# Attention logits in two row halves, with the forget-gate bias and the causal mask in one tile

## The chip, the cores and the metric

The kernel runs on one core of one Trainium2 chip, as one program launched once. The metric is the device time in microseconds of one execution; times are medians of several runs. One further execution is recorded by the hardware profiler, and all rows below are from such executions.

## The reference

A decoder of two layers over 256 tokens of width 1024, all in float32. Each layer is a feed-forward at half step, a token mixer and another feed-forward at half step, with RMSNorm in front of and behind each. The mixer of the first layer is a gated linear recurrence. That of the second is "forgetting" attention with 16 heads of 64, whose keys, values and gates are computed from the stream between the layers:

```python
def shared_kv(h, g, w_kv, w_f, b_f):
    hn = rms_norm(h, g)
    kv = (hn @ w_kv)            # keys and values, 16 heads of 64
    log_f = log_sigmoid(hn @ w_f + b_f)
    c = cumsum(log_f, axis=1)   # running sum over the tokens, per head
...
    logits = q @ k + c[query] - c[key]
    logits = where(key <= query, logits, -inf)
    p = softmax(logits)
    o = p @ v
```

## The kernel before

The 256 tokens are two row tiles of 128, called t = 0 and t = 1. Every large product splits both operands into a high and a low part and adds three products of the parts (lines L183 to L185). The high part of a weight is an ACT copy (L173), the low part a DVE subtraction (L177). The weights arrive through the SP queue into five `raw` buffers, and nine pairs of split buffers (`WB = 9`) let the splits run ahead of PE.

The work is a list of items, each with a `prep` (load and split) and a `work` (the products for one row tile). `slot(t, i)` does item i for tile t. `run` walks the list, tile 1 some `LAG = 7` slots behind tile 0. `ahead(i, fn)` makes item i's prep call `fn` first. `defer(n, fn)` calls `fn` n slots later. PE's instructions stay in the order in which they are written. The other engines' order is settled when the program is built, by a planner that takes what is ready first, by its own estimates; on the chip each of them then works through its list in order. `keep_in_program_order` pins an instruction behind the one written before it on the same engine.

The stages that the change touches, in the order of time:

- Between the layers, keys, values and gates. `post_f` makes the log gates `lf`. Fifteen slots later `running(t)` sums them on PE with a triangle of ones, with heads on partitions: `c` is 16x128. A DMA lays `c` into row 65 of the key tile `kT`, whose row 64 is ones. `heads_T` scales the 512 columns of a projection (`htok`, L954), two slots later transposes them four times (L959), and copies the lower 64 partitions by ACT (L962) and the upper 64 by DVE (L963), so that every head lies on partitions 0 to 63.
- The first feed-forward of the second layer. Its last items are the 22 rows of the down projection. Its gate and up products use two buffers with the tag `sil`. At its end, `enter` computes the norm: sums of squares on ACT, `rstd` on POOL (L198, L200), the new `h` on DVE (L285), and PE's transposes of `h` (L214).
- The attention. `att_rows` lays `c` and minus one into rows 64 and 65 of the query tiles `qT`, by four POOL DMAs (L947, L948), so that a product of 66 rows holds query times key plus both running sums. The steps of the attention are laid by hand between the slots of the query and output projections (`ATT_ORDER`): `l` logits, `n` norm, `t` transposes (L1084), `v` values (L1098), each followed by its row tile. One `l` does a group of heads that fills one of two `gt` PSUM banks: four heads of 128 keys for tile 0, two of 256 for tile 1 (L1063). DVE adds the mask to the diagonal block (L1064) and takes the maximum (L1066), ACT takes the exponential head by head with its sum (L1071).

A float32 product of these small ones goes through PE in two passes, so the row counts of L1063 are twice the number of products.

Of the kernel before, what the change touches and what calls it, by code (L numbers as in the profile page):

```python
# [23 lines left out]
NRT = 11  # L24
NH = 16
HD = 64
HA = HD + 2
EPS = 1e-6
RAW = 5
WB = 9  # L30
# [14 lines left out]
def trunk_kernel(ctx: ExitStack, tc: tile.TileContext, A: dict, out: bass.AP):  # L45
# [6 lines left out]
    hpool = ctx.enter_context(tc.tile_pool(name="h", bufs=1))  # L52
    spool = ctx.enter_context(tc.tile_pool(name="small", bufs=4))
    psum = ctx.enter_context(tc.tile_pool(name="psum", bufs=1, space=bass.MemoryType.PSUM))

    uid = [0]

    def nm(s):
        uid[0] += 1
        return f"{s}_{uid[0]}"  # L60
# [4 lines left out]
    def gtbank():  # L65
        return psum.tile([P, 512], F32, tag="gt", name=nm("gt"), bufs=2)
# [850 lines left out]

    def kv_tiles():
        lp = ctx.enter_context(tc.tile_pool(name="kv", bufs=1, reuse_waits="tile"))
        kv["kT"] = lp.tile([HA, NH, S], F32, name="kT")  # L920
        kv["v"] = [lp.tile([P, D], F32, name=f"v{t}") for t in range(2)]

        kv["lf"] = [lp.tile([P, NH + 8], F32, name=f"lf{t}")[:, :NH] for t in range(2)]
        kv["c"] = [lp.tile([NH, P], F32, name=f"c{t}") for t in range(2)]
        kv["bfb"] = lp.tile([P, NH], F32, name="bfb")
        for n in ("triu", "mone", "cmask"):
            kv[n] = lp.tile([P, P], F32, name=n)

    def kv_constants():

        keep = tc.keep_in_program_order
        triu, cm = kv["triu"], kv["cmask"]
        keep(nc.gpsimd.dma_start(kv["bfb"], A["b_fgate"].partition_broadcast(P)))
        keep(nc.gpsimd.memset(triu, -1.0))
        keep(nc.gpsimd.affine_select(out=triu, in_=triu, compare_op=ALU.is_ge, fill=0.0, base=0,
                                     pattern=[[1, P]], channel_multiplier=-1))
        keep(nc.gpsimd.memset(kv["mone"], -1.0))
        keep(nc.gpsimd.memset(cm, 0.0))
        keep(nc.gpsimd.affine_select(out=cm, in_=cm, compare_op=ALU.is_ge, fill=NEG, base=0,
                                     pattern=[[-1, P]], channel_multiplier=1))  # L940
        keep(nc.gpsimd.memset(kv["kT"][HD:HA, :, :], 1.0))
# [8 lines left out]
    def heads_T(pool, ps, t, n, scale, dst):  # L950

        tok = pool.tile([P, 512], F32, tag="prod", name=nm("htok"), bufs=2)
        with tc.high_priority():
            nc.vector.tensor_scalar(tok, ps, rs[t][:, 0:1], scale, ALU.mult, ALU.mult)  # L954

        def turn():
            tp = trbank()
            for j in range(4):
                nc.tensor.transpose(tp[:, j * P:(j + 1) * P], tok[:, j * P:(j + 1) * P], ident)  # L959
            to = dst[:HD, 8 * n:8 * n + 8, :].rearrange("p (a two) b -> p a two b", two=2)  # L960
            with tc.high_priority():
                nc.scalar.activation(to[:, :, 0, :], tp[:HD, :].rearrange("p (a b) -> p a b", a=4), AF.Copy)  # L962
                nc.vector.tensor_copy(to[:, :, 1, :], tp[HD:, :].rearrange("p (a b) -> p a b", a=4))  # L963
        defer(2, turn)

    def post_k(n):
        return lambda t, ps: heads_T(pools["f"], ps, t, n, 1.0, kv["kT"][:, :, t * P:(t + 1) * P])

    def post_f(t, ps):
        fp = pools["f"]  # L970
# [15 lines left out]
        rest()  # L986

    def running(t):
        pc = gtbank()
        if t == 1:  # L990
            nc.tensor.matmul(pc[:NH, :P], kv["lf"][0], kv["mone"], start=True, stop=False)
        nc.tensor.matmul(pc[:NH, :P], kv["lf"][t], kv["triu"], start=t == 0, stop=True)
        nc.vector.tensor_copy(kv["c"][t], pc[:NH, :P])
        nc.gpsimd.dma_start(kv["kT"][HD + 1:HA, :, t * P:(t + 1) * P], kv["c"][t])

    def z_x(t, k):
        return zx[t][0][:, k, :], zx[t][1][:, k, :]
# [33 lines left out]
    for n in range(2):  # L1031
# [11 lines left out]

    def att_tiles():
        ap = pools["a"]
        att["q"] = [ap.tile([HA, NH, P], F32, name=f"qT{t}") for t in range(2)]
        att["oh"] = [ap.tile([P, 8, P], F32R, name=f"oh{t}") for t in range(2)]
        att["ol"] = [ap.tile([P, 8, P], F32R, name=f"ol{t}") for t in range(2)]

    def attention(t):  # L1050

        ap = pools["a"]
        nk = t + 1
        per = 4 // nk
        mask = kv["cmask"].unsqueeze(1).to_broadcast([P, per, P])
        box = {}
        G = NH // per

        def logits(hg):
            hds = range(hg * per, (hg + 1) * per)  # L1060
            ps = gtbank().rearrange("p (a b) -> p a b", a=per)
            for j, hd in enumerate(hds):
                nc.tensor.matmul(ps[:, j, :], att["q"][t][:, hd, :], kv["kT"][:, hd, :nk * P], start=True, stop=True)  # L1063
            nc.vector.tensor_tensor(ps[:, :, t * P:], ps[:, :, t * P:], mask, ALU.add)  # L1064
            mx = spool.tile([P, 4], F32, tag="mx", name=nm("mx"))
            nc.vector.tensor_reduce(mx[:, :per], ps, AX.X, ALU.max, negate=True)  # L1066
            if hds[0] % 8 == 0:
                box["sm"] = spool.tile([P, 8], F32, tag="sm", name=nm("sm"))
            pe = ap.tile([P, per, nk * P], F32, tag="pe", name=nm("pe"), bufs=3)
            for j, hd in enumerate(hds):  # L1070
                nc.scalar.activation(pe[:, j, :], ps[:, j, :], AF.Exp, bias=mx[:, j:j + 1],  # L1071
                                     accum_out=box["sm"][:, hd % 8:hd % 8 + 1])
            box["pe", hg], box["s", hg] = pe, box["sm"][:, hds[0] % 8:hds[0] % 8 + per]

        def norm(hg):
            pe, sm = box["pe", hg], box["s", hg]
            nc.vector.reciprocal(sm, sm)
            nc.vector.tensor_tensor(pe, pe, sm.unsqueeze(2).to_broadcast([P, per, nk * P]), ALU.mult)

        def turn(hg):  # L1080
            tp = trbank()
            pev = box["pe", hg].rearrange("p a b -> p (a b)")
            for j in range(4):
                nc.tensor.transpose(tp[:, j * P:(j + 1) * P], pev[:, j * P:(j + 1) * P], ident)  # L1084
            pT = box["pT", hg] = ap.tile([P, 4, P], F32, tag="pT", name=nm("pT"), bufs=4)
            nc.scalar.activation(pT.rearrange("p a b -> p (a b)"), tp, AF.Copy)

        def values(hg):

            hds = range(hg * per, (hg + 1) * per)  # L1090
            if hds[0] % 8 == 0:
                box["po"] = mmbank()
            po, pT = box["po"].rearrange("p (a b) -> p a b", a=4), box["pT", hg]
            for j in range(0, per, 2):
                for k in range(nk):
                    for s in range(2):
                        hd = hds[j + s]
                        nc.tensor.matmul(po[s * HD:(s + 1) * HD, hd % 8 // 2, :], kv["v"][k][:, hd * HD:(hd + 1) * HD],  # L1098
                                         pT[:, (j + s) * nk + k, :], start=k == 0, stop=k == nk - 1)
            if hds[-1] % 8 == 7:  # L1100
                b = hds[-1] // 8
                oh_v = att["oh"][t][:, 4 * b:4 * b + 4, :].rearrange("p a b -> p (a b)")
                ol_v = att["ol"][t][:, 4 * b:4 * b + 4, :].rearrange("p a b -> p (a b)")
                nc.scalar.activation(oh_v, box["po"], AF.Copy)
                nc.vector.tensor_tensor(ol_v, box["po"], oh_v.bitcast(F32), ALU.subtract)

        return {c: [lambda i=i, f=f: f(i) for i in range(G)] for c, f in zip("lntv", (logits, norm, turn, values))}

    def post_q(n):
        return lambda t, ps: heads_T(pools["a"], ps, t, n, HD ** -0.5, att["q"][t])  # L1110

    for n in range(2):
        proj_items(A["attn_w_q"][0], n * 512, 512, main_x, post_q(n))
# [246 lines left out]
```

## Time and profile before

| | |
|---|---|
| median of three runs | 987.53 us (987.33 to 987.55) |
| the profiled execution | 987.51 us, its span 985.8 us |
| granted clock of TensorE | 0.998 |
| busy: PE, DVE, ACT, POOL | 978.0, 616.6, 530.1, 47.2 us |
| DMA, mean over the span | 193 GB/s, 190.45 MB |

A row of a view gives the line of the kernel, the engine, the operation, the tiles (out<-in), shapes and times; "x8" is a count, and the bracket at the end is the engine's idle time before it and what ended it. PE is matmul, PEld the weight load that overlaps it, DVE the vector engine, ACT the scalar engine, POOL GpSimd, SP the queue that issues most DMAs. In the chain of work, a piece has its start, its length up to the next piece, the engine and the line. A row of the table of windows has, for each engine, busy time and count, then the granted clock, the share of the DMA engines and GB/s. A row of the DMA queues has packets, MB and the share of 16 engines' span. A row of the DMA issues has KB and the median time from issue to landing.

### The profile page before, as it was taken

To read this page: it belongs to the slowest core of one execution; us is meant where nothing else is said; L and a number is where in the kernel's file an instruction comes from. 1 tells how busy PE (TensorE), PEld (TensorE's weight loads), DVE (VectorE), ACT (ScalarE), POOL (GpSimd) and SP (SyncE) were. 2 spreads that over 40 slices of the span, in tenths; PEclk is the share of its full clock that TensorE was granted. 3 is DMA by queue.
4 is the path that set the end of the run, shared out by engine and by line. 5 is a ranking of instruction groups with operands and counts; after the bars stand their busy time and mean duration, and the time that the engine had idled before them with its cause. 6 is when DMAs were issued, how large, how long until landed. Compare 5 with 4: busy or idle time off the path is not lost.

```text
span 985.8 us, 13028 instructions
## 1 busy us (share of the span) xinstructions
PE 978.0 (99%) x4777; PEld 813.4 (83%) x4777; DVE 616.6 (63%) x791; ACT 530.1 (54%) x753; POOL 47.2 (5%) x92
## 2 busy tenths in 40 slices
PE   9999999999999999999999999999999999999997
PEld 6888888898978888888898888888888788888886
DVE  6666554678997555554686655554488876555542
ACT  7545443568986544443564444544366755444431
POOL 2400000100003000000100000000020000000000
PEclk9999999999999999999999999999999999999999
DMA  8787766565346877666567676665552467776631
GB/s 292 263 266 249 222 210 192 158 192 162 117 126 198 241 211 212 217 207 188 131 203 242 186 220 213 214 213 185 190 173 64 123 210 235 213 213 212 205 117 43
DMA packets 99558, 190.45 MB, mean 193 GB/s; under 512 B 12734, under 2 KB 32614, under 8 KB 99494
## 3 DMA queue, kind: packets, MB, share of 16 engines
q1 hardware_dynamic: 98054, 188.95, 61.3%
q8 instruction: 38, 0.62, 0.3%
q10 hardware_dynamic: 608, 0.53, 0.2%
q0 software_dynamic: 832, 0.12, 0.1%
q14 instruction: 26, 0.21, 0.1%
HBM read 176.95 MB, written 1.05 MB: 181 GB/s over the span
## 4 chain that ended last, share of the span: by engine, by line
PE 98%; issue 1%; DVE 1%; ACT 0%; POOL 0%; POOLq 0%; DVEq 0%; ACTq 0%
PE mm L183 29%; PE mm L185 29%; PE mm L184 28%; PE gt L761 2%; PE tr L525 1%; PE mm L1195 1%; PE gt L1063 1%; PE mm L190 1%; PE mm L191 1%; PE mm L192 1%; PE mm L1098 1%; PE tr L1084 1%; PE gt L214 1%; PE tr L127 0%; PE tr L959 0%
## 5 line engine op out<-in xcount | busy, mean ns | idle before, releaser
L177 DVE TENSOR_TENSOR wlo<-raw,whi 128x1024 fp32r<-128x1024 f32 (+5 forms) x329 | 395.3, 1207 | 268.3 <-ACT whi L173 266.1
L173 ACT ACTIVATE whi<-raw 128x1024 fp32r<-128x1024 f32 (+5 forms) x329 | 341.9, 1046 | 314.8 <-PE mm L185 260.2
L183 PE MATMUL mm<-whi,xhi 128*128 128x512 f32 (+1 forms) x768 | 301.2, 392 | 0.0
L185 PE MATMUL mm<-whi,xlo 128*128 128x512 f32 (+1 forms) x768 | 298.2, 388 | 0.3 <-DVE xlo L228 0.3
L184 PE MATMUL mm<-wlo,xhi 128*128 128x512 f32 (+1 forms) x768 | 297.9, 388 | 0.0
L185 PEld LDWEIGHTS mm<-whi,xlo 128*128 128x128 f32 x768 | 144.2, 188 | 30.7 <-DVE xlo L228 0.7
L183 PEld LDWEIGHTS mm<-whi,xhi 128*128 128x128 f32 x768 | 144.2, 188 | 29.4 <-issue 1.3
L184 PEld LDWEIGHTS mm<-wlo,xhi 128*128 128x128 f32 x768 | 144.3, 188 | 28.2 <-DVE wlo L177 0.3
L183 PE MATMUL mm<-whi,hhi 128*128 128x512 f32 x352 | 137.9, 392 | 0.0
L185 PE MATMUL mm<-whi,hlo 128*128 128x512 f32 x352 | 137.1, 389 | 0.0
L184 PE MATMUL mm<-wlo,hhi 128*128 128x512 f32 x352 | 137.0, 389 | 0.0
L185 PEld LDWEIGHTS mm<-whi,hlo 128*128 128x128 f32 x352 | 66.1, 188 | 13.9
L184 PEld LDWEIGHTS mm<-wlo,hhi 128*128 128x128 f32 x352 | 66.1, 188 | 13.3
L183 PEld LDWEIGHTS mm<-whi,hhi 128*128 128x128 f32 x352 | 66.1, 188 | 13.3
L510 DVE SCALAR_TENSOR_TENSOR prod<-mm,rstd,sil 128x512 f32<-128x512 f32 (+1 forms) x48 | 33.8, 705 | 35.2 <-PE mm L185 31.1
L498 ACT ACTIVATE sil<-mm,rstd 128x512 f32<-128x512 f32 (+1 forms) x48 | 31.2, 651 | 38.7 <-PE mm L185 34.2
L198 POOL TENSOR_SCALAR nv<-ss 128x1 f32<-128x1 f32 x22 | 9.6, 435 | 716.3 <-ACT junk L205 716.3
L529 ACT ACTIVATE hhi<-tr 128x512 fp32r<-128x512 f32 (+1 forms) x48 | 24.8, 558 | 13.8 <-PE tr L525 13.8
L205 ACT ACTIVATE junk<-mm 128x512 bf16<-128x512 f32 x24 | 14.3, 595 | 32.7 <-PE mm L185 32.6
L272 DVE TENSOR_TENSOR t<-mm,gb 128x512 f32<-128x512 f32 x24 | 16.1, 685 | 24.7 <-ACT junk L205 24.6
L530 DVE TENSOR_TENSOR hlo<-tr,hhi 128x512 fp32r<-128x512 f32 (+1 forms) x48 | 29.2, 640 | 2.6 <-ACT hhi L529 2.6
L183 PE MATMUL mm<-whi,zhi 128*128 128x340 f32 (+2 forms) x80 | 28.2, 353 | 0.0
(196 smaller groups left out, 885.8 us busy)
## 6 DMA issues: line engine op xcount, KB each, us to landing
raw<-in_ffn_w_down_dram SPq DMA_DIRECT2D x88, 512.0 KB
raw<-in_ffn_w_up_dram SPq DMA_DIRECT2D x80, 512.0 KB
raw<-in_ffn_w_gate_dram SPq DMA_DIRECT2D x78, 512.0 KB
prr<-prod SPq DMA_DIRECT2D x40, 256.0 KB
raw<-in_rg_w_in_dram SPq DMA_DIRECT2D x10, 504.0 KB
raw<-in_rg_w_out_dram SPq DMA_DIRECT2D x10, 504.0 KB
raw<-in_ffn_w_gate_dram SPq DMA_DIRECT2D x19, 256.0 KB
raw<-in_ffn_w_up_dram SPq DMA_DIRECT2D x16, 256.0 KB
```

Of the source, the lines that this page charges most:

```text
L173: up = nc.scalar.activation(hi[:parts, c:c + m], rawv[:, c:c + m], AF.Copy)
L177: nc.vector.tensor_tensor(lo[:parts, c:c + m], rawv[:, c:c + m], hi[:parts, c:c + m].bitcast(F32), ALU.subtract)
L183: nc.tensor.matmul(ps, xh, wh, start=first, stop=False)
L184: nc.tensor.matmul(ps, xh, wl, start=False, stop=False)
L185: nc.tensor.matmul(ps, xl, wh, start=False, stop=last)
L205: nc.scalar.activation(junk[:, :src.shape[1]], src, AF.Square, scale=f, accum_out=acc)
L272: nc.vector.tensor_tensor(t1[n], pf[n], gb[:, n * 512:(n + 1) * 512], ALU.mult)
L498: nc.scalar.activation(s[:, :nn], ps, AF.Silu, scale=rs[t][:, 0:1])
L510: nc.vector.scalar_tensor_tensor(pr[:, :nn], ps, rs[t][:, 0:1], s, ALU.mult, ALU.mult)
L529: nc.scalar.activation(hv, tp[:, :nn], AF.Copy)
L530: nc.vector.tensor_tensor(lv, tp[:, :nn], hv.bitcast(F32), ALU.subtract)
L761: nc.tensor.matmul(ps[j][:w, g * S:(g + 1) * S], wv[rows, o:o + w], xc[rows, k, :], start=start, stop=stop, skip_group_check=True)
```

## The change

Keys and queries stay as the transposes leave them: two heads on the two halves of the 128 partitions, copied once by ACT. A product of logits has 64 rows, and the even heads (rows 0 to 63) and odd heads (64 to 127) go to two PSUM banks. One `l` step does two groups, the next one nothing. Mask and running sums are no longer in the product: they are a bias tile, added when the maximum is taken, in one DVE instruction per head that also writes the (negated) sum to SBUF for the exponential.

For that, `running` computes the sums a second time with tokens on partitions (`cq`) and writes the sums with heads on partitions to DRAM (`rows`). A bias over four heads and 128 keys is made by three steps: a POOL DMA spreads four of these rows over all partitions, DVE subtracts `cq`, and for a diagonal block POOL puts the mask in. The bias of tile 0 is made in `running(0)` and stays in SBUF. That of tile 1 (2 MB) is made in eight parts in the tail of the feed-forward in front of the attention, in the two `sil` buffers, and each part is written to DRAM; `att_rows` loads all of it by one DMA.

```diff
     def kv_tiles():
-        kv["kT"] = lp.tile([HA, NH, S], F32, name="kT")
+        kv["kT"] = lp.tile([P, NH // 2, S], F32, name="kT")
...
+        kv["cq"] = [lp.tile([P, NH], F32, name=f"cq{t}") for t in range(2)]
+        kv["bias0"] = lp.tile([P, NH, P], F32, name="bias0")
+        kv["rows"] = dram.tile([NH, S], F32, name="crows")
+        kv["bias1"] = dram.tile([P, NH, S], F32, name="bias1d")
...
+    def bias_of(v, t, h0, masked):
+        nc.vector.tensor_tensor(v, v, kv["cq"][t][:, h0:h0 + 4].unsqueeze(2).to_broadcast([P, 4, P]), ALU.subtract)
+        if masked:
+            tc.keep_in_program_order(
+                nc.gpsimd.affine_select(out=v, in_=v, compare_op=ALU.is_ge, fill=NEG, base=0,
+                                        pattern=[[0, 4], [-1, P]], channel_multiplier=1))
+
+    def key_rows(v, h0, k):
+        tc.keep_in_program_order(nc.gpsimd.dma_start(v, kv["rows"][h0:h0 + 4, k * P:(k + 1) * P].partition_broadcast(P)))
+
+    def bias_part(i):
+        h0, k = i // 2 * 4, i % 2
+        def f():
+            v = pools["f"].tile([P, 512], F32, tag="sil", name=nm("bp"), bufs=2).rearrange("p (a b) -> p a b", a=4)
+            key_rows(v, h0, k)
+            bias_of(v, 1, h0, k == 1)
+            tc.keep_in_program_order(nc.gpsimd.dma_start(kv["bias1"][:, h0:h0 + 4, k * P:(k + 1) * P], v))
+        return f
...
     def att_rows():
-        for t in range(2):
-            tc.keep_in_program_order(nc.gpsimd.dma_start(att["q"][t][HD:HD + 1, :, :], kv["c"][t]))
-            tc.keep_in_program_order(nc.gpsimd.dma_start(att["q"][t][HD + 1:HA, :, :], kv["mone"][:NH, :]))
+        tc.keep_in_program_order(nc.gpsimd.dma_start(att["bias1"], kv["bias1"]))
...
     def heads_T(...):
-                nc.scalar.activation(to[:, :, 0, :], tp[:HD, :].rearrange("p (a b) -> p a b", a=4), AF.Copy)
-                nc.vector.tensor_copy(to[:, :, 1, :], tp[HD:, :].rearrange("p (a b) -> p a b", a=4))
+                nc.scalar.activation(dst[:, 4 * n:4 * n + 4, :], tp.rearrange("p (a b) -> p a b", a=4), AF.Copy)
...
     def running(t):
...
+        if t == 1:
+            nc.tensor.matmul(pq[:, :NH], one, kv["lf"][0], start=True, stop=False)
+        nc.tensor.matmul(pq[:, :NH], kv["triu"], kv["lf"][t], start=t == 0, stop=True)
...
+        nc.vector.tensor_copy(kv["cq"][t], pq[:, :NH])
+        nc.gpsimd.dma_start(kv["rows"][:, t * P:(t + 1) * P], ct)
+        if t == 0:
+            for h0 in range(0, NH, 4):
+                key_rows(kv["bias0"][:, h0:h0 + 4, :], h0, 0)
+                bias_of(kv["bias0"][:, h0:h0 + 4, :], 0, h0, True)
...
+    for i in range(8):
+        ahead(n_ffn3 - 10 + i, bias_part(i))
...
         def logits(hg):
-            hds = range(hg * per, (hg + 1) * per)
-            ps = gtbank().rearrange("p (a b) -> p a b", a=per)
-            for j, hd in enumerate(hds):
-                nc.tensor.matmul(ps[:, j, :], att["q"][t][:, hd, :], kv["kT"][:, hd, :nk * P], start=True, stop=True)
-            nc.vector.tensor_tensor(ps[:, :, t * P:], ps[:, :, t * P:], mask, ALU.add)
-            nc.vector.tensor_reduce(mx[:, :per], ps, AX.X, ALU.max, negate=True)
+            if hg % 2:
+                return
+            ps = [gtbank() for _ in range(2)]
...
+            for hd in range(h0, h0 + 2 * per):
+                r = slice(hd % 2 * HD, (hd % 2 + 1) * HD)
+                nc.tensor.matmul(logit(hd), att["q"][t][r, hd // 2, :], kv["kT"][r, hd // 2, :w], start=True, stop=True,
+                                 skip_group_check=True)
...
+            for g in (hg, hg + 1):
+                for j, hd in enumerate(hds):
+                    nc.vector.tensor_tensor_reduce(pe[:, j, :], logit(hd), bias[:, hd, :], -1.0, -NEG, ALU.add, ALU.min,
+                                                   mx[:, j:j + 1])
+                for j, hd in enumerate(hds):
+                    nc.scalar.activation(pe[:, j, :], pe[:, j, :], AF.Exp, bias=mx[:, j:j + 1], scale=-1.0,
+                                         accum_out=box["sm"][:, hd % 8:hd % 8 + 1])
```

More of the change, by code (lines that the diff above doesn't have):

```diff
@@ L26 @@
 HD = 64
-HA = HD + 2
 EPS = 1e-6
@@ L925, in kv_tiles @@
         kv["bfb"] = lp.tile([P, NH], F32, name="bfb")
-        for n in ("triu", "mone", "cmask"):
-            kv[n] = lp.tile([P, P], F32, name=n)
+        kv["triu"] = lp.tile([P, P], F32, name="triu")
+        kv["one"] = lp.tile([P, 32], F32, name="one")[:, :1]
+        kv["bias0"] = lp.tile([P, NH, P], F32, name="bias0")
+        kv["rows"] = dram.tile([NH, S], F32, name="crows")
+        kv["bias1"] = dram.tile([P, NH, S], F32, name="bias1d")
     def kv_constants():
         keep = tc.keep_in_program_order
-        triu, cm = kv["triu"], kv["cmask"]
+        triu = kv["triu"]
@@ L933, in kv_constants @@
         keep(nc.gpsimd.dma_start(kv["bfb"], A["b_fgate"].partition_broadcast(P)))
-        keep(nc.gpsimd.memset(triu, -1.0))
+        keep(nc.gpsimd.memset(triu, 1.0))
         keep(nc.gpsimd.affine_select(out=triu, in_=triu, compare_op=ALU.is_ge, fill=0.0, base=0,
                                      pattern=[[1, P]], channel_multiplier=-1))
[L937 to L940, printed above, removed]
@@ L941, in kv_constants @@
-        keep(nc.gpsimd.memset(kv["kT"][HD:HA, :, :], 1.0))
+        keep(nc.gpsimd.memset(kv["one"], 1.0))
+    def bias_of(v, t, h0, masked):
[4 more added lines that the diff above has]
+                                        pattern=[[0, 4], [-1, P]], channel_multiplier=1))
@@ L953, in heads_T @@
+    def heads_T(pool, ps, t, n, scale, dst, tag, bufs):
+        tok = pool.tile([P, 512], F32, tag=tag, name=nm("htok"), bufs=bufs)
         with tc.high_priority():
@@ L1045, in att_tiles @@
         ap = pools["a"]
-        att["q"] = [ap.tile([HA, NH, P], F32, name=f"qT{t}") for t in range(2)]
+        att["q"] = [ap.tile([P, NH // 2, P], F32, name=f"qT{t}") for t in range(2)]
+        att["bias1"] = ap.tile([P, NH, S], F32, name="bias1")
         att["oh"] = [ap.tile([P, 8, P], F32R, name=f"oh{t}") for t in range(2)]
@@ L1054, in attention @@
         per = 4 // nk
-        mask = kv["cmask"].unsqueeze(1).to_broadcast([P, per, P])
+        bias = kv["bias0"] if t == 0 else att["bias1"]
+        w = nk * P
         box = {}
```

34 lines of the change are left out of this document (17 added, 17 removed).

## The prediction

> **What bounds the kernel now.** I read the page's busy times and its chain of work first, then the pieces of that chain in the attention and around the steps that the change moves, then the rows of DVE and POOL there.
>
> ```profile
> span 985.8 us, 13028 instructions
> PE 978.0 (99%) x4777; PEld 813.4 (83%) x4777; DVE 616.6 (63%) x791; ACT 530.1 (54%) x753; POOL 47.2 (5%) x92
> PE 98%; issue 1%; DVE 1%; ACT 0%; POOL 0%; POOLq 0%; DVEq 0%; ACTq 0%
> ```
>
> TensorE (PE) is busy for 978.0 of 985.8 us and 98% of the chain is PE. So a change gains only what it takes off PE's own queue. It loses whatever PE has to wait for, because PE works in order and nothing is slack behind it. The profiled execution took 987.51 us, 1.7 more than its span, and the median of the three timed runs is 987.53: the sum below can be made against either.
>
> **What the row halves take off PE.** In the chain, one group of logits (L1063) of the first row tile is 8 passes over 128 columns, one of the second is 4 passes over 256.
>
> ```profile
> 738.49 0.89 PE gt L1063 x8
> 760.50 0.44 PE tr L1084 x4
> 765.45 0.86 PE gt L1063 x4
> 766.31 1.02 PE mm L1098 x16
> 767.34 0.59 PE tr L1084 x4
> ```
>
> A whole pass takes 0.111 us (0.89/8) or 0.215 us (0.86/4). The price of half-height passes is in the same trace twice. The values (L1098) use two column halves: 16 passes of 128 columns take 1.02 us, 0.064 each, and the transposes behind them 0.59 in place of 0.44. The gates of the first layer (L761) use two row halves, as the change does, on 256 columns:
>
> ```profile
> 221.01 2.79 PE gt L761 x16
> 223.80 0.43 PE mm L183
> 224.23 0.23 PE mm L184
> ```
>
> Eight of these 16 passes are whole (8 x 0.215 = 1.72), eight are halves. Of 2.79 us, and 0.20 that the next matmul is late (0.43 for 0.23), the halves have 1.27 us.
>
> After the change two groups run in one call. A call for the first row tile has 16 half passes of 128 columns: 1.02 + 0.15 = 1.17 us against 2 x 0.89 = 1.78, so 0.61 saved, and there are two calls: 1.2 us. A call for the second tile has eight half passes of 256 columns, just L761's eight: 1.27 against 2 x 0.86 = 1.72, so 0.45 saved, times four calls: 1.8 us. Together 3.0 us.
>
> **What the running sums add to PE.** They are computed a second time with tokens on partitions: one fp32 product of 16 columns for tile 0 and two for tile 1, six passes.
>
> ```profile
> 529.89 0.32 PE gt L991 x2
> L1063 PEld LDWEIGHTS gt<-kT,qT x64: 186/190/192, 734.4 to 776.1; 66*128 66x128 f32 x64
> ```
>
> No row has so few moving columns against 128 stationary ones. If only the moving columns count, a pass is an eighth of 0.11 us, 0.1 in all; if the weight load is bare, it is 0.19, 1.1 in all. I take the pace of small fp32 passes, 0.11 (0.44/4 for L1084): 0.7 us. **PE's own sum is 3.0 - 0.7 = 2.3 us off: 985.2 us**, with bounds 984.6 and 985.6 from these prices.
>
> **DVE and ACT in the attention.** Mask add and maximum go; one fused instruction per head comes.
>
> ```profile
> L1064 DVE TENSOR_TENSOR gt<-gt,cmask x12: 410/432/699, 735.8 to 776.8; 128x256 f32<-128x256 f32 x8, 128x512 f32<-128x512 f32 x4
> L1066 DVE TENSOR_REDUCE mx<-gt x12: 666/683/691, 736.5 to 777.8; 128x2 f32<-128x512 f32 x8, 128x4 f32<-128x512 f32 x4
> L1071 ACT ACTIVATION_READ_ACCUMULATOR pe<-gt,mx x32: 192/200/224, 737.6 to 779.4; 128x1 f32 x32
> L963 DVE COPY qT<-tr x4: 692/693/693, 734.1 to 763.8; 64x512 f32<-64x512 f32 x4
> 740.00:750.00 10.00, 10.00 (x65) 8.48 (x64) 9.06 (x13) 6.45 (x21) 0.00 (x0) 1.00 0.44 121
> ```
>
> Gone: 4 x (0.70 + 0.68) + 8 x (0.43 + 0.68) = 14.4 us and four copies of qT, 2.8 us. The fused instruction is not in the trace. As one pass like L1064's it is 0.30 on 128 columns (the line through 0.43 and 0.70) and 0.43 on 256: 16 x 0.30 + 16 x 0.43 = 11.7 us. If its sum is read out separately, as ACT's is in 0.20, it is 18.1. So DVE, 9.06 busy of 10 us here, ends between 5.5 us lighter and 0.9 heavier. I take the lighter half, since two PSUM passes become one, and no PE time. The exponentials read SBUF for PSUM, count unchanged; both banks are free sooner because the exponentials no longer hold them. A DVE that is heavier instead is a rival below. The kT and qT copies on ACT keep their size in columns; nothing waits for the DVE halves any more.
>
> **What the bias tile adds in front.** This is where I see the danger. Eight parts each do: a POOL DMA that spreads four rows of 128 over 128 partitions (256 KB), a DVE subtraction, for every second part a POOL select over 128x512, and a POOL DMA of 256 KB to DRAM. All of a part's POOL instructions are pinned behind the ones before. So part i+1 cannot ask for its rows until part i's have landed and DVE is through. One round is a full DMA latency, and eight rounds are serial. Their rows:
>
> ```profile
> bfb<-in_b_fgate_dram POOLq DMA_DIRECT2D x1, 8.0 KB, 4.2
> qT<-c POOLq DMA_DIRECT2D x2, 8.0 KB, 5.8
> q1 hardware_dynamic: 98054, 188.95, 61.3%
> q10 hardware_dynamic: 608, 0.53, 0.2%
> L994 POOL DMA_DIRECT2D kT<-c x2: 490/546/603, 520.1 to 531.0; - x2
> L935 POOL TENSOR_SCALAR_AFFINE_SELECT triu<-triu x1: 990/990/990, 312.7 to 312.7; 128x128 f32<-128x128 f32 x1
> ```
>
> A small POOL DMA lands in 4.2 us (a broadcast) to 5.8. The part's 512 packets of 512 B are 32 for each of 16 DMA engines. A packet takes 0.10 us on the big queue (61.3% of 16 x 985.8 us by 98054) and 0.05 on the small one: 1.7 to 3.2 us more. The landing is then 5.9 to 9.0 us. With a subtraction of 0.69 (L1064's 128x512 form), an issue of 0.5 and half a select (0.99 for 128 columns; up to four times that for 512), a round is 7.6 to 12.2 us. I take 7.6: the queues stand at 0.6 here.
>
> The rows use the gate buffers (tag sil, two of them), which this layer's last gate product reads until here:
>
> ```profile
> 667.59 0.48 DVE L510 SCALAR_TENSOR_TENSOR prod<-mm,rstd,sil 128x256 f32<-128x256 f32 x1 [0.73 <-ACT sil L498]
> 687.43 1.23 DVE L177 TENSOR_TENSOR wlo<-raw,whi 128x1024 fp32r<-128x1024 f32 x1 [1.50 <-ACT whi L173]
> 690.15 1.23 DVE L177 TENSOR_TENSOR wlo<-raw,whi 128x1024 fp32r<-128x1024 f32 x1 [1.49 <-ACT whi L173]
> 714.39 0.30 POOL L198 TENSOR_SCALAR nv<-ss 128x1 f32<-128x1 f32 x1 [182.85 <-ACT junk L205]
> 714.77 0.56 POOL L200 TENSOR_TENSOR rstd<-nv,mhalf 128x1 f32<-128x1 f32 x1
> 715.37 1.42 DVE L285 SCALAR_TENSOR_TENSOR h<-t,rstd,h 128x512 f32<-128x512 f32 x2 [0.36 <-POOL rstd L200]
> 717.59 0.87 PE gt L214 x8
> ```
>
> From 668.1 us, eight rounds of 7.6 end at 729. But at 714.4 POOL has to compute rstd of tile 0 (L198, L200). DVE's h (L285) waits for that, and PE's transposes (L214) for h: h is done at 716.79, PE starts at 717.59. That chain has 0.80 us to spare. Two things are queued behind a late part: on POOL the rstd, and on DVE the low halves of the weights (L177), since DVE too works in an order fixed at build. L177 comes every 2.72 us, after 1.5 us of idle time, and of the nine split buffers about five lie between tile 0 and tile 1, so the splits run some four units ahead of PE: an estimate of 11 us of cover. So DVE's queue can bear one late part but not a growing lag; POOL's rstd can bear 0.8 us.
>
> How many parts stand in front of the rstd in POOL's queue is the planner's choice, which no row shows. None gives 0; all eight give 729 - 714.4 - 0.8 = 13.8 us. I take one round, since rounds are long and the planner can only put the rstd between two of them: 7.6 - 0.8 = 6.8 us. **The sum is 985.2 + 6.8 = 992.0 us.**
>
> The rest I cost at nothing. Four such rounds for tile 0's bias run on POOL from 520 us; their DVE steps could hold up the key projection:
>
> ```profile
> 542.07 0.75 DVE L954 TENSOR_SCALAR htok<-mm,rstd 128x512 f32<-128x512 f32 x1 [0.40 <-PE mm L185]
> 544.76 0.44 PE tr L959 x4
> 753.17 0.86 PE gt L1063 x4
> ```
>
> The htok that PE transposes is done 1.9 us ahead; a subtraction waiting for its rows longer than that would add the excess, at most a round. The one 2 MB load of the bias is issued after 726 in place of four small ones. At the page's mean of 193 GB/s it is about 11 us long, and its first reader follows the logits at 753: covered, unless the last part is later than about 738.
>
> **A rule against my forecast.** The Trainium skill, "DMA: Bandwidth & Descriptors", section "Anatomy of one DMA — SWDGE (gpsimd) path", gives such a DMA 2.0 us plus its bytes over 436 GB/s: an estimate of 2.6 us for 256 KB. By it a round would be 4.3 us, the eight would end at 702, and the sum would be 985.2. The rows here have 4.2 to 5.8 us for 8 KB alone, so I go by them.
>
> **The rivals.** *The gain comes through: 985.2 us.* If 256 KB land as fast as the 8 KB broadcast (4.2 us), a round is 5.9 us and eight end at 715, just as the rstd is wanted. Or the planner sees the rounds as long as they are and puts the rstd and the weights first; then only the load at 738 remains as a limit. The point that decides is a landing of 4.2 us, or POOL's order. For it: DVE and ACT have idle time in this stretch. Against it: every POOL DMA in the trace is at 4.2 us or above when other queues move. The skill's fit above falls under this rival.
>
> *All parts stand in front: 999 us and above.* Eight rounds of 7.6 give 985.2 + 13.8 = 999.0; rounds of 8.1 give 1003. For it: between 572 and 714 POOL has nothing else, so nothing stops the planner from starting early.
>
> *The attention eats it: 987.5 us.* If the fused instruction costs 0.20 more, DVE is 0.9 us heavier where it is 9.06 of 10 busy, and transposes wait; a loss of 2.3 us would balance PE's gain. The same result would follow if the two row halves did not run side by side; L761 speaks against that.
>
> **How the numbers follow.** The forecast has 0.42, the gain that comes through 0.36, all parts in front 0.15, the eaten gain 0.07. About 0.2% (2 us) is what a measurement here can tell from no change. Of the rival at 985.2, whose bounds reach 985.6, 0.33 lies below 985.55 and is faster; 0.03 of it and the eaten gain are the same, 0.10; the rest is slower, 0.57. The forecast by itself reaches from 988 (half a round late) to 998. The range goes to both sides of that, from 984.4, just under the gain that comes through, to 1003, so that the slowest rounds alone are left out.
>
> **What would show it.** Right: L1063 at about 1.2 us a call in place of 1.7 to 1.8; landings of the rows at 6 us or more; a DVE subtraction that waits for a DMA; rstd later than 715 and idle time of PE at L214, or at a split, worth about 7 us. Wrong: landings near 4 us, or rstd in time with parts behind it. Then PE stays at 99% without a gap and the time is near 985. PE idle in the attention with DVE full would mean the fused instruction.

## The result and the profile after

The changed kernel takes 1015.51 us (median of 4 runs, 1014.43 to 1016.2); the kernel before took 987.54 beside it. The ratio is 1.0282, with a 95% interval of 1.0264 to 1.03. The forecast was 992.0, with a range of 984.4 to 1003.0: the direction is right, the size is outside the range.

The profiled execution took 1015.15 us. From its page, in this order: span, busy times, the granted clock in 40 slices of the span, and the chain that ended last.

```profile
span 1013.3 us, 13121 instructions
...
PE 985.0 (97%) x4783; PEld 813.3 (80%) x4783; DVE 617.0 (61%) x837; ACT 531.0 (52%) x753; POOL 69.8 (7%) x114
...
PEclk9999999999999999999998999999889999999999
...
PE 85%; issue 6%; DMA 4%; DVE 2%; POOL 1%; ACT 1%; POOLq 0%; DVEq 0%; ACTq 0%
```

The span is 27.5 us longer. PE's share of the chain falls from 98% to 85%: DMA, issue and DVE are on it now. And the clock line, 9 throughout before, has three slices of 8, one in the key projection and two near the end of the feed-forward. Three stages of work move the time. I compared the start of the same product (every L183, counted from the first) in both traces: at the last product ahead of the key projection the changed kernel is 0.7 us late, behind that projection 10.9, where the attention begins about 30.6, and at the end 27.6. So: **+10.2 in the key projection, +19.7 in the tail of the feed-forward, -3.0 in the attention.** (The running sums have 0.2 of the first 0.7 us and 0.5 of the 10.2.)

The waits of the changed kernel that are new or longer (engine, line, what it waited for: us in total, times, longest):

```profile
DVE bp L944 <- DMA bp<-crows: 24.0, 5, 5.9
POOL bias1d L960 <- DVE bp L944: 22.6, 4, 6.1
DVE bias L944 <- DMA bias<-crows: 17.3, 4, 5.7
DVE bp L944 <- issue: 15.8, 3, 5.4
PE mm L184 <- DVE wlo L177: 10.6, 3, 6.5
PE tr L977 <- DVE htok L972: 7.7, 2, 5.6
```

The first and third lines are the new subtraction standing on DVE until its rows have landed. The fourth is the same subtraction in the three other rounds of the tail; the profile shows no releaser for them, but they are as long as the rest. In the tail that makes eight waits, 39.8 us. The last two are PE standing for DVE: for the low halves of weights (L177) in the tail, and for htok in the key projection. PE never waits for a new tile itself. It waits for old work that is queued behind the new.

The transfers by kind (queue, count, KB each, median us from issue to landing):

```profile
bp<-crows POOLq DMA_DIRECT2D x8, 256.0 KB, 5.5
bias1d<-bp POOLq DMA_DIRECT2D x8, 256.0 KB, 3.8
bias<-bias1d POOLq DMA_DIRECT2D x1, 2048.0 KB, 11.7
bias<-crows POOLq DMA_DIRECT2D x4, 256.0 KB, 4.8
```

A row spread lands in 4.8 to 5.5 us. The Trainium skill, "DMA: Bandwidth & Descriptors", section "Anatomy of one DMA — SWDGE (gpsimd) path", gives 2.0 us plus bytes over 436 GB/s, an estimate of 2.6 us for 256 KB: here the measurement is about twice that, and it decides. The 2 MB load took 11.7 us and nothing waited for it.

**The key projection.** DVE's timeline (start, us, operation, idle time before and who ended it):

```profile
538.66 0.69 DVE L944 TENSOR_TENSOR bias<-bias,cq 128x512 f32<-128x512 f32 x1 [3.55 <-DMA bias<-crows]
...
540.68 0.73 DVE L972 TENSOR_SCALAR htok<-mm,rstd 128x512 f32<-128x512 f32 x1
```

and PE's around it and in the tail:

```profile
535.49 0.39 PE L185 MATMUL mm<-whi,zlo 128*128 128x512 f32 x1
541.47 1.12 PE L977 MATMUL tr<-ident,htok 128*128 128x128 f32 x4 [5.59 <-DVE htok L972]
542.24 0.78 PE L183 MATMUL mm<-whi,zhi 128*128 128x512 f32 x1
...
555.38 0.66 PE L977 MATMUL tr<-ident,htok 128*128 128x128 f32 x4 [2.13 <-DVE htok L972]
...
716.15 0.39 PE L183 MATMUL mm<-whi,hhi 128*128 128x512 f32 x1
719.55 0.79 PE L184 MATMUL mm<-wlo,hhi 128*128 128x512 f32 x1 [3.02 <-DVE wlo L177]
720.15 0.63 PE L185 MATMUL mm<-whi,hlo 128*128 128x512 f32 x1
720.57 0.63 PE L183 MATMUL mm<-whi,hhi 128*128 128x512 f32 x1
...
725.69 0.42 PE L183 MATMUL mm<-whi,hhi 128*128 128x512 f32 x1
725.95 0.39 PE L184 MATMUL mm<-wlo,hhi 128*128 128x512 f32 x1
...
736.93 0.80 PE L184 MATMUL mm<-wlo,hhi 128*128 128x512 f32 x1 [6.54 <-DVE wlo L177]
...
747.27 1.32 PE L214 MATMUL gt<-ident,h 128*128 128x128 f32 x8 [1.40 <-DVE h L285]
```

The projection's last products before the gap start at 535.49; the htok they lead to is computed only at 540.68, because DVE stands at the second subtraction until 538.66, and has that, two small copies and the split of a weight to do first. PE is idle for 5.59 us. A second gap of 2.13 follows at 553.25: 7.7 us in all. After the gap PE is also slow for a while, which is seen best in the tail: after 719.55 products follow each other by 0.42 to 0.43 us (720.15 to 720.57), and only from 725.69 by 0.23 to 0.26 again. The same stretches in the windows (PE, PEld, DVE, ACT, POOL busy, then granted clock, DMA share, GB/s):

```profile
540.00:550.00 10.00, 8.53 (x33) 7.12 (x34) 4.82 (x5) 2.73 (x3) 4.79 (x5) 0.76 0.38 90
...
720.00:730.00 10.00, 8.94 (x27) 6.46 (x26) 4.04 (x4) 2.12 (x2) 3.12 (x4) 0.71 0.62 179
730.00:740.00 10.00, 3.46 (x9) 2.48 (x8) 1.83 (x2) 0.69 (x2) 1.60 (x3) 0.63 0.62 204
```

Before, the clock was 1.00 in each of these. The Trainium skill, "TensorE: Matmul & The Clock Gate", section "Part 1: The HAM clock gate (the "warmup" mystery)", states that an idle array falls back to half its clock, that 512-column products then start 426.7 ns apart, and that some 3.4 us of sustained work releases it. The 0.427 us here agrees; the release took about 3 us in the key projection and about 6 in the tail.

**The tail.** POOL's timeline: its first part, its last, and the rstd. Between them, ACT's last sum of squares that this rstd needs.

```profile
679.25 0.77 POOL L951 DMA_DIRECT2D bp<-crows  x1 [124.09 <-DVE prod L510]
...
740.80 0.60 ACT L205 ACTIVATE junk<-mm 128x512 bf16<-128x512 f32 x1 [1.93 <-PE mm L185]
...
742.73 1.55 POOL L947 TENSOR_SCALAR_AFFINE_SELECT bp<-bp 128x512 f32<-128x512 f32 x1 [5.21 <-DVE bp L944]
744.58 0.78 POOL L960 DMA_DIRECT2D bias1d<-bp  x1 [0.29 <-POOL bp L947]
745.39 0.31 POOL L198 TENSOR_SCALAR nv<-ss 128x1 f32<-128x1 f32 x1
```

All eight parts stand in POOL's queue in front of tile 0's rstd (L198). From 679.25 to 745.39 they take 66.1 us, 8.27 a round. Without this delay the rstd would have been due near 724.85 (its time in the kernel of experiment 5 below): it is 20.5 us late, and less the 0.8 us that it had to spare, that is the 19.7 us of this stage.

POOL is not alone in this. By the comparison of starts, PE is 10.9 us late ahead of the gaps at L177 and 28.3 us behind them and their slow products (at 742.95). So 17.4 us are gone before PE first stands for h, and only 1.40 us are left to wait at L214. PE's lateness also delays the data of the rstd itself: the last sum of squares is done at 741.5, less than 4 us before POOL is through. Each of the two queues, DVE's and POOL's, is late enough for most of the loss, and POOL's ends last. With the rstd ahead of the parts in POOL's queue, some 16 of the 19.7 us would have stayed. That is an estimate from these rows; no run tried it.

**The attention**, in the chain (start, us, line), the one gap of PE there, and the groups of the fused instruction (min/median/max ns):

```profile
774.47 1.09 PE gt L1101 x16
782.51 1.06 PE gt L1101 x8
```

```profile
806.54 0.66 PE L1140 MATMUL mm<-pT,v 128*64 128x128 f32 x8 [0.55 <-ACT pT L1128]
```

```profile
L1110 DVE CUSTOM_DVE_ANT_0 pe<-gt,bias x32: 260/348/425, 766.6 to 805.8; 128x128 f32<-128x128 f32 x16, 128x256 f32<-128x256 f32 x16
L1110 DVE DVE_READ_ACCUMULATOR2_ANT mx<- x32: 82/83/85, 766.8 to 806.2; 128x1 f32 x32
```

Calls are 1.09 and 1.06 us where 1.17 and 1.27 were expected. The fused instruction takes 0.26 and 0.43, plus 0.083 for reading out. At 806.54 PE waits for ACT's copy of the transposes; by the comparison of starts 0.8 us are lost there.

### The profile page after: what moved, and what is told of

It reads as the page before. It is cut to its first block, busy times and chain, and to the rows that moved or that the text cites. A ratio compares the mean times of both kernels' runs of the same rounds, so it can differ in the third digit from the quotient of the medians.

```text
span 1013.3 us, 13121 instructions
## 1 busy us (share of the span) xinstructions
PE 985.0 (97%) x4783; PEld 813.3 (80%) x4783; DVE 617.0 (61%) x837; ACT 531.0 (52%) x753; POOL 69.8 (7%) x114
## 4 chain that ended last, share of the span: by engine, by line
PE 85%; issue 6%; DMA 4%; DVE 2%; POOL 1%; ACT 1%; POOLq 0%; DVEq 0%; ACTq 0%
PE mm L183 25%; PE mm L185 25%; PE mm L184 25%; DMA bias<-crows 2%; PE gt L761 1%; PE tr L525 1%; DMA bp<-crows 1%; DVE wlo L177 1%; PE mm L190 1%; PE mm L191 1%; PE mm L192 1%; DMA raw<-in_ffn_w_up_dram 1%; PE gt L214 1%; PE gt L1101 1%; PE mm L1140 1%
## 5 line engine op out<-in xcount | busy, mean ns | idle before, releaser
L177 DVE TENSOR_TENSOR wlo<-raw,whi 128x1024 fp32r<-128x1024 f32 (+5 forms) x329 | 397.4, 1215 | 241.0 <-ACT whi L173 238.7
L183 PE MATMUL mm<-whi,xhi 128*128 128x512 f32 (+1 forms) x768 | 301.1, 392 | 0.0
L183 PEld LDWEIGHTS mm<-whi,xhi 128*128 128x128 f32 x768 | 144.2, 188 | 29.5 <-issue 1.3
L184 PE MATMUL mm<-wlo,hhi 128*128 128x512 f32 x352 | 140.0, 398 | 10.6 <-DVE wlo L177 10.6
L183 PE MATMUL mm<-whi,hhi 128*128 128x512 f32 x352 | 139.8, 397 | 0.0
L185 PE MATMUL mm<-whi,hlo 128*128 128x512 f32 x352 | 139.3, 396 | 0.0
L183 PEld LDWEIGHTS mm<-whi,hhi 128*128 128x128 f32 x352 | 67.4, 192 | 13.9
L198 POOL TENSOR_SCALAR nv<-ss 128x1 f32<-128x1 f32 x22 | 9.7, 442 | 537.2 <-ACT junk L205 537.2
L944 DVE TENSOR_TENSOR bp<-bp,cq 128x512 f32<-128x512 f32 x8 | 5.5, 693 | 39.8 <-DMA bp<-crows 24.0
```

Source lines behind the costliest of these rows:

```text
L177: nc.vector.tensor_tensor(lo[:parts, c:c + m], rawv[:, c:c + m], hi[:parts, c:c + m].bitcast(F32), ALU.subtract)
L183: nc.tensor.matmul(ps, xh, wh, start=first, stop=False)
L184: nc.tensor.matmul(ps, xh, wl, start=False, stop=False)
L185: nc.tensor.matmul(ps, xl, wh, start=False, stop=last)
```

## Theory, rivals and experiments

The theory: PE's own sum is as forecast, near 985; all of the loss is made by the two chains of row spreads, one in the key projection through DVE's queue, one in the tail through POOL's. The rivals: something else in the change costs time (the attention, the layout); DVE's waits by themselves starve the weights in the tail; contention of the transfers; the slow clock.

**1. Both chains out.** The biases are zeros, written early, so mask and running sums are left out of the logits.

```diff
-            for h0 in range(0, NH, 4):
-                key_rows(kv["bias0"][:, h0:h0 + 4, :], h0, 0)
-                bias_of(kv["bias0"][:, h0:h0 + 4, :], 0, h0, True)
...
-    for i in range(8):
-        ahead(n_ffn3 - 10 + i, bias_part(i))
```

> The changed kernel with neither bias chain: tile 0's bias is a tile of zeros, tile 1's is loaded from zeros written to DRAM early (running sums and mask are left out of the logits); row halves, fused maximum, running's extra products and the 2 MB load stay. Theory (the time is lost where DVE waits in order for the spread rows, at the key projection and in the tail of the feed-forward): 985.2 us, PE's own sum, L977 and the splits without gaps. Rival (the attention itself got dearer, or the 2 MB load disturbs the weights): 990 or more. Rival (PE's clock fell for another reason than the waits): the granted clock stays at 0.99 and the time near 995.

Measured: 985.48 us (985.03 to 987.39), ratio 0.9976 (0.9966 to 0.9986). The forecast for PE's own sum was 985.2. No gap is left at L177 or at the htok transposes. Everything lost is in the chains.

**2. Tile 1's parts out, tile 0's chain kept.** The bias of tile 1 is zeros.

```diff
-    for i in range(8):
-        ahead(n_ffn3 - 10 + i, bias_part(i))
```

> Tile 0's bias chain stays, the eight parts for tile 1 are left out (tile 1's bias is zeros from DRAM). Theory: the two chains cost by themselves, so the feed-forward's tail gives its 19.2 us back and the key projection keeps its 10.2: 996.3 us. Rival (the second chain was late only because the first had delayed everything, or both share one cause): below 990 or above 1005.

Measured: 995.31 us (993.31 to 995.56), ratio 1.0072 (1.0056 to 1.0088). The waits of this kernel (its lines are three further on):

```profile
PE tr L980 <- DVE htok L975: 7.2, 2, 5.5
```

995.31 - 985.48 = 9.8 us for tile 0's four rounds, of which 7.2 are PE's gaps. From the first of these gaps on, PE's products are 0.43 us apart for about 4.6 us, which is most of the rest.

**3. The subtraction on POOL.** Nothing is left out; DVE no longer stands in front of a landing.

```diff
-        nc.vector.tensor_tensor(v, v, kv["cq"][t]...
+        tc.keep_in_program_order(nc.gpsimd.tensor_tensor(v, v, kv["cq"][t]...
```

> The changed kernel with the subtraction of the running sum moved from DVE to POOL, for both tiles; nothing left out. Only POOL then waits for landings. Theory (DVE's queue holds the weights' low halves and htok): the gaps at L977 and at the splits vanish, the key projection gives back 10 us; but the rounds are as serial and about 1 us longer, so now POOL's rstd of the feed-forward's end is the late one: parts end near 740, about 25 us after it is wanted, PE's gap moves to the transposes of h (L214), and the time is 1005 to 1015. Rival (rstd does not wait behind the parts): 985 to 990. Rival (DMA contention, not queue order, delays the weights): gaps at the splits stay, 1015.

Measured: 1007.82 us (1005.65 to 1008.8), ratio 1.02 (1.0184 to 1.0216). PE's only long gap, and POOL's rows that end it:

```profile
728.97 0.75 POOL L951 DMA_DIRECT2D bp<-crows  x1
...
736.39 0.31 POOL L198 TENSOR_SCALAR nv<-ss 128x1 f32<-128x1 f32 x1
...
738.20 1.97 PE L214 MATMUL gt<-ident,h 128*128 128x128 f32 x8 [19.79 <-DVE h L285]
```

The gaps at htok and L177 are gone, and with them the loss in the key projection. The tail's loss stays, in one piece: eight parts, then the rstd, then h, then PE. By the starts of the products it is 22.3 us here: the gap and some slow products behind it. So POOL's queue alone is enough for it. Whether DVE's waits alone would be, with all eight rounds and the rstd in time, no run shows.

**4. The same with four parts.** Heads 8 to 15 of tile 1 have no bias; the subtraction is on POOL.

```diff
-    for i in range(8):
+    for i in range(4):
```

> As the kernel with the subtraction on POOL, but with the first four of the eight parts only (heads 8 to 15 of tile 1 get zeros: running sums and mask are left out for them). Theory (the rounds are serial, about 8.3 us each, and the rstd stands behind all of them): four end at about 669 + 4 x 8.3 = 702, before POOL's rstd is wanted at 714, so the 19.8 us gap at the transposes of h vanishes altogether and the time is 985 to 986. Rival (a gap that falls in proportion to the bytes moved, by contention): about 996.

Measured: 985.08 us (985.02 to 985.27), ratio 0.9972 (0.996 to 0.9983).

```profile
707.24 0.78 POOL L963 DMA_DIRECT2D bias1d<-bp  x1 [0.29 <-POOL bp L950]
715.02 0.31 POOL L198 TENSOR_SCALAR nv<-ss 128x1 f32<-128x1 f32 x1 [7.00 <-ACT junk L205]
```

POOL is through at 708, six microseconds later than expected, and then idle for 7.00 us until the rstd's own data come, at 715.02. The same spreads by the same queue cost nothing when they end in time, and in experiment 3 all eight of them left no split of a weight late: contention of the transfers is out as a cause.

**5. Four parts, subtraction on DVE as in the change** (against the kernel of experiment 4; heads 8 to 15 again without their bias).

```diff
-        tc.keep_in_program_order(nc.gpsimd.tensor_tensor(v, v, kv["cq"][t]...
+        nc.vector.tensor_tensor(v, v, kv["cq"][t]...
```

> The changed kernel with only the first four of tile 1's eight parts (heads 0 to 7; the bias of heads 8 to 15 in DRAM is filled with zeros early, so it is left out), and the subtraction on DVE as in the change. It parts the tail's loss into POOL's queue and DVE's waits. Theory (in the tail DVE's landings cost nothing by themselves as long as the lag stays inside the cover of some 11 us; the loss there came from eight rounds of 8.2 us): four rounds from 679 end at 712, ahead of the rstd; only the key projection's loss is left, about 9.8 us as with all parts out: 994.5 to 996. Rival (DVE's waits starve the splits from the first rounds on): gaps of PE at the splits, L177, of several us, 998 to 1003.

Measured: 995.09 us (994.24 to 996.07), ratio 1.0075 (1.006 to 1.009).

```profile
PE tr L980 <- DVE htok L975: 5.6, 2, 4.9
...
710.24 0.50 PE L184 MATMUL mm<-wlo,hhi 128*128 128x512 f32 x1 [0.28 <-DVE wlo L177]
...
710.98 0.78 POOL L963 DMA_DIRECT2D bias1d<-bp  x1 [0.30 <-POOL bp L950]
...
724.85 0.30 POOL L198 TENSOR_SCALAR nv<-ss 128x1 f32<-128x1 f32 x1 [13.09 <-ACT junk L205]
```

This is the time of experiment 2: the key projection's loss and almost nothing else. DVE stands for four landings in the tail, and PE has one gap of 0.28 us at a split, in the fourth round. So the cover there just holds for four rounds. In the changed kernel the first gap at a split begins at 716.5, in the fifth round.

**6. One load for tile 0's rows** in place of four.

```diff
+            tc.keep_in_program_order(nc.gpsimd.dma_start(kv["bias0"], kv["rows"][:, :P].partition_broadcast(P)))
             for h0 in range(0, NH, 4):
-                key_rows(kv["bias0"][:, h0:h0 + 4, :], h0, 0)
```

> The changed kernel; only tile 0's rows come by one DMA of 1 MB in place of four of 256 KB, one pinned behind the other; nothing left out. Theory (the key projection waits for the second to fourth serial round): one landing is left, about 8 to 9 us after its issue at 526, that is 535; DVE may wait for it once, before htok is needed at 535, and the key projection loses 0 to 4 us in place of 10.2: 1005 to 1010. Rival (POOL's selects, or the load's bytes, hold the stage up): still 1013 or more.

Measured: 1015.52 us (1014.92 to 1017.2), ratio 1.0281 (1.0267 to 1.0295): no gain, which was not expected.

```profile
536.78 3.38 DVE L944 TENSOR_TENSOR bias<-bias,cq 128x512 f32<-128x512 f32 x4 [8.22 <-DMA bias<-crows]
...
544.02 1.12 PE L977 MATMUL tr<-ident,htok 128*128 128x128 f32 x4 [7.91 <-DVE htok L972]
```

The four subtractions now stand together in front of htok, and DVE waits for them 8.22 us in one go. PE's idle time is 7.91 us for 7.7. The load's bytes have a part in it: it landed 10.4 us after its issue, where 8 to 9 were expected. Thus it is not the serial rounds as such that hurt in the key projection, but that DVE's queue has a subtraction, whose rows are still on the way, ahead of an htok that PE needs.

**7. PE kept busy over the gap.** 25 products on constants ahead of the first htok transposes.

```diff
+            if (tag, t, n) == ("prod", 0, 0):
+                keep_busy(25)
```

> The changed kernel with 25 dummy bf16 products of 512 columns on PE in front of the key projection's first transposes, where PE has a gap of 5.6 us (they take about 5.3 us); nothing left out. Theory (PE's granted clock falls because PE stood idle): the granted clock between 540 and 550 us is 1.00 in place of 0.76, and the stage is about 2.5 us shorter: 1013. Rival (the clock falls for another reason, such as load on the die): granted clock as before, 1015.5 or a little more.

Measured: 1017.97 us (1012.71 to 1018.76), ratio 1.0292 (1.0268 to 1.0316). The window of its trace:

```profile
540.00:550.00 10.00, 10.00 (x48) 7.98 (x47) 2.07 (x3) 3.78 (x4) 2.69 (x3) 1.00 0.49 154
```

The clock is 1.00 where the changed kernel has 0.76, so it was the idle time that lowered it. The profiled execution is the one of 1012.71; the three timed ones are 1017.3 to 1018.8, no better than the change. In the profiled one PE leaves the key projection 1.5 us earlier than in the change. What the slow clock costs there by itself is not settled by this run. In the tail it should gain little, since there the rstd is late anyway; that was not tried.

**8. Rows spread straight into the attention's tile.** A term that is the same for all keys of a query cancels in the softmax, so the subtraction and its products go; four loads bring the rows of all 256 keys into the SBUF tile, POOL masks them there, and the parts and the copy in DRAM go.

```diff
-        nc.vector.tensor_tensor(v, v, kv["cq"][t]...
...
-        tc.keep_in_program_order(nc.gpsimd.dma_start(att["bias1"], kv["bias1"]))
+        for h0 in range(0, NH, 4):
+            v = att["bias1"][:, h0:h0 + 4, :]
+            tc.keep_in_program_order(nc.gpsimd.dma_start(v, kv["rows"][h0:h0 + 4, :].partition_broadcast(P)))
...
+        for a in range(4):
+            defer(7 + a, lambda a=a: mask(4 * a))
...
-        kv["cq"] = [lp.tile([P, NH], F32, name=f"cq{t}") for t in range(2)]
```

> No subtraction and no parts: a constant per query does not change a softmax, so the bias is the key's running sum alone. Tile 0's rows are spread and masked on POOL; tile 1's are spread straight into the attention's tile by four DMAs of 512 KB where the 2 MB load was, and masked there on POOL. running's products for the query side go too. Theory: DVE and rstd wait for nothing; PE's sum of 3.0 us for the row halves is all that is left, 984.5 us. Rival (four rounds on POOL at the key projection hold something up by themselves): 988 or more, with gaps between 530 and 560. Rival (the spread rows land too late for the second tile's logits at 751): a gap in the attention.

Measured: 990.36 us (989.97 to 990.55), ratio 1.0025 (1.0015 to 1.0035); 984.5 was expected. PE has no gap left at htok, at the splits or at the transposes of h. The page's busy line, and its group of the down projection's products (busy, mean ns):

```profile
PE 979.8 (99%) x4777; PEld 808.6 (82%) x4777; DVE 608.5 (62%) x823; ACT 530.6 (54%) x753; POOL 53.9 (5%) x101
...
L183 PE MATMUL mm<-whi,hhi 128*128 128x512 f32 x352 | 139.4, 396 | 0.0
```

The products of the second to fourth down projection are a little slower, spaced by 0.232 to 0.233 us instead of 0.227. Those of the first are at 0.227 as before.

**9. The same with the two tiles of 64 bytes put back,** so that later tiles keep their places; they are set to zero once and not used. The masks come three slots later.

```diff
+        kv["cq"] = [lp.tile([P, NH], F32, name=f"cq{t}") for t in range(2)]
...
-            defer(7 + a, lambda a=a: mask(4 * a))
+            defer(10 + a, lambda a=a: mask(4 * a))
```

> The kernel without subtraction and parts, with two unused 64-byte tiles put back in place of the query sums (so that all later tiles lie at the addresses they have in the changed kernel) and the masks of tile 1 three slots later. Theory (the 990.4 us came from where the down projection's stationary tiles lie: there PE took 0.232 us a product for 0.227, without any gap): 984.5 us, products back at 0.227. Rival (the POOL work in the attention or the missing products are the cause): 990 again.

Measured: 984.76 us (984.64 to 984.97), ratio 0.9968 (0.9956 to 0.9981).

```profile
PE 974.1 (99%) x4777; PEld 807.8 (82%) x4777; DVE 608.7 (62%) x823; ACT 530.8 (54%) x753; POOL 53.3 (5%) x103
...
L183 PE MATMUL mm<-whi,hhi 128*128 128x512 f32 x352 | 137.8, 392 | 0.0
```

The same 4777 products are busy for 5.7 us less, about the 5.6 us of the difference.

**10. The two tiles, with the masks at their first place** (7 + a), which parts the two edits of experiment 9.

```diff
-            defer(10 + a, lambda a=a: mask(4 * a))
+            defer(7 + a, lambda a=a: mask(4 * a))
```

> The version with the rows spread straight into the attention's tile and the two unused 64-byte tiles kept, with the masks on POOL three slots earlier than there, as in the version without the two tiles. The two versions, 990.36 and 984.76, differed in both things. Theory (where the later tiles lie sets the pace of the down projection's products): 984.5 to 985.2, products at 0.227 us. Rival (POOL's masks three slots earlier cost it): about 990, products at 0.232.

Measured: 984.64 us (984.34 to 985.07), ratio 0.9967 (0.9956 to 0.9979). It was the two tiles, not the masks' time. That they act through the places of the tiles behind them is the likely reading, but no trace shows the places. Experiments 8 to 10 leave nothing out, and 9 and 10 are 2.9 and 3.0 us faster than the kernel before, which is what the row halves save.

## Why the prediction was wrong

**Right: PE's sum.** 3.0 us less in the attention were forecast and the trace has 3.0; without the chains the kernel takes 985.48 against 985.2. The rival that the attention eats the gain falls with it. That the two figures are equal is in part luck. The calls cost less than forecast (1.09 and 1.06 us), so by themselves they save 2 x 0.69 + 4 x 0.66 = 4.0, and 0.8 of that is lost again at 806.54, where PE waits for ACT. The fused instruction, 9.7 us in all plus 2.7 for reading out, lies between the two bounds given.

**Right: where the danger lies.** Rstd behind parts in POOL's queue, splits behind landings in DVE's, landings of about 6 us, and the load of 11 us that stays covered: all are in the trace.

**Wrong, the first step, in the tail:** "I take one round, since rounds are long and the planner can only put the rstd between two of them". It put none between: all eight stand in front. This was the rival with a chance of 0.15. Nothing in the profile of before spoke for one round over eight; the rival's own argument, that POOL has nothing else from 572 on, was the better one. The price of the rival was too low as well, 13.8 us for 19.7. A round has 8.27 us and not 7.6: the landing is shorter than assumed (5.5), but the two issues cost 0.75 to 0.78 each and the select 1.55 with 0.29 ahead of it. Eight times 0.67 is 5.3 of the 5.9 us that are missing. The other 0.7 is that the chain began 11.2 us later (679.25 for 668.1) and the rstd was wanted 10.5 later (724.85 for 714.4), both after the key projection's loss.

The same step put nothing in the sum for DVE in the tail. "DVE's queue can bear one late part but not a growing lag" was right. With four rounds PE has one gap of 0.28 us at a split (experiment 5); with eight, gaps of 10.6 us begin in the fifth round, and 17.4 of the 19.7 us are lost that way and by the slow products behind, before POOL's late rstd is felt. So the rival with all parts in front priced one queue where two were late.

**Wrong, the step that cost 9.8 us more:** "The rest I cost at nothing". The htok was known to be 1.9 us ahead and the excess was put at no more than a round; the first gap alone is 5.59 us, and a second of 2.13 follows. The landing of 4.8 us was already in the prediction's rows as 5.9 or more, so a subtraction planned just ahead of htok had to be late. The prediction asked on POOL who stands behind a late landing, and did not ask it again on DVE for these four.

**Not in the sum at all:** a PE that has stood goes on at half pace. It adds about 2 us in the key projection by the trace (10.2 less 7.7 of gaps and 0.5 of running sums). In the tail it lies inside the lateness of the rstd.

**A misread row, of no consequence:** "every POOL DMA in the trace is at 4.2 us or above when other queues move". The eight small loads that POOL issues between 23.6 and 27.1 us in the kernel before land in 3.7 and 3.8 us (medians of four each), with the DMA engines 0.96 busy. The medians of the row spreads, 4.8 and 5.5, are above 4.2 all the same.

By these sizes the sum would have been 985.2 + 9.8 + 19.7 = 1014.7, against 1015.51 measured. The last two terms are read from runs of the change, so this shows only that nothing large is missing.

## What to carry to other kernels

A chain of transfers that runs through in-order queues is priced by what stands behind each of its waits, on every engine that it touches; the first question is how many of its links the order puts in front of the next critical instruction, and if no row answers that, all of them is the case to forecast. Moving the consumer of a slow landing to an engine with nothing urgent behind it gave back the key projection's loss here, and doing away with it (the subtraction cancels in the softmax) left no such loss at all; one load in place of four gave nothing. A gap of PE of 3 us or more is counted with some microseconds at half pace behind it, unless something later is late anyway.

## What the runs showed of the hardware that was not expected

A gap of 3.02 us was enough for PE to fall to 0.427 us per 512-column product, for about 6 us; after one of 1.06 us it stayed near 0.23, and so it did after 2.73 us in the kernel of experiment 7. The slow pace need not begin with the first product: after gaps of 3.57 and 3.19 us in the tails of experiments 6 and 7, PE ran at its old pace for 1.3 us and only then fell to 0.427, for 3.4 us. And two unused tiles of 64 bytes per partition ahead of the others matter to PE, probably by where the others then lie: without them the products of three of the four down projections are spaced by 0.232 to 0.233 us in place of 0.227, and the kernel is 5.6 us longer. Which of the tiles behind them is sensitive, and why, was not tried.
